# Selection of 16 experts a head with tiles and keys innermost, 17 dense chunks for 19, and sends at two of three token groups

## The chip, the core and the metric

The kernel runs on one core of a Trainium2 chip, as one launch. The core has five engines with a queue each: TensorE (PE; its weight loads are told apart as PEld), VectorE (DVE), ScalarE (ACT), GpSimd (POOL) and SyncE (SP), which here issues most transfers; DMA engines move the data. The metric is the device time of one execution in microseconds (us), the median of several runs; less is better.

## The reference, cut to what matters

Two transformer blocks on 256 tokens of width 1024. The first two thirds of the kernel (attention, convolution, state space, feed-forward, and a second mixer) are not touched. The change lies in the last layer, a feed-forward over 16384 experts, of which every token takes 16 for each of 8 heads:

```python
def retrieve(xb):                       # 128 tokens
    q = (xb @ wq).reshape(PEER_BLOCK, PEER_HEADS, 2, PEER_QDIM // 2)
    s = jnp.einsum('tphq,phkq->tphk', q, keys)          # 2 x 128 keys a head
    top_s, top_i = lax.top_k(s, PEER_TOPK)              # 16 of each 128
    cand = top_s[:, :, 0, :, None] + top_s[:, :, 1, None, :]
    best_s, best_c = lax.top_k(cand.reshape(PEER_BLOCK, PEER_HEADS, 256), PEER_TOPK)
    i1 = jnp.take_along_axis(top_i[:, :, 0], best_c // PEER_TOPK, axis=-1)
    i2 = jnp.take_along_axis(top_i[:, :, 1], best_c % PEER_TOPK, axis=-1)
    idx = i1 * PEER_NKEYS + i2
    g = jax.nn.softmax(best_s, axis=-1)
    act = jax.nn.gelu(jnp.einsum('tpkd,td->tpk', u_tab[idx], xb), approximate=False)
    return jnp.einsum('tpk,tpkd->td', g * act, v_tab[idx])
```

The two take_along_axis lines are what the changed part of `topk` computes: which key number stands at each of the 16 best places.

## The kernel before, in words

An expert's number is 128 times a first key plus a second key. The kernel splits the second keys into D dense ones and 128 - D sparse ones. For the dense keys, u·x is computed for all 128 x D experts and all tokens, two keys to a "chunk"; for the sparse keys only experts that some token chose are gathered. `peer` (L1627) has five stages:

- **Selection** (L1807 to L1816). `head(h)` multiplies the queries of head h on PE (`dense`, L1685: 16 matmuls on 1 MB that SP loads in two halves), multiplies them with the keys (L1708), and ACT copies the scores to the tile sc, of which there are two. `topk` (L1477) then works on DVE alone: per tile of 128 tokens it takes the 16 best of each 128 keys (L1490 to L1494), adds the 16 x 16 pairs (L1497), takes the 16 best (L1503 to L1507), and splits each place into two numbers from 0 to 15 (L1509, L1510). For both tiles and both keys together, L1516 to L1518 turn the places into key numbers: compare each place with 0 to 15 (the table io16, made once on POOL), multiply by the key numbers, add up over the 16. `chunk()` (L1780) is one dense chunk, placed between heads: 16 more matmuls, and a Gelu on ACT.
- **Weights** (L1714): softmax on DVE and ACT, and transposes of idx and of the weights on PE (L1731).
- **Token groups** (L1819): 64 groups of 4 tokens. DVE makes one-hot rows (L1752, L1753), ACT copies one set (L1754), PE multiplies them to the weights of all 16384 experts for each token (L1767, L1769); DVE multiplies those of the keys whose chunk is done into A (L1773) and ACT copies the rest there (L1774). Every tenth group has a chunk. `keep` (L1792) sends eight keys of one tile of A to the DRAM tables Gd (sparse) and Ad (dense), L1802, in SP's queue, each behind the last load.
- **Listing** (`listing`, L1521): the experts with a weight above 0 are numbered, those of the first tile alone, of both, and of the second alone in turn, and turned into lists of 128 to a column, in blocks of four pairs of keys (L1586 to L1597, DVE, ACT and PE in turn). `lims` (L1635) holds for the sparse and the dense keys the column from which the second tile takes part, the column up to which the first does, and the number of columns. The chunks that are left and the other sends come here too.
- **Last stage** (L1854 to L2002): 33 steps of two columns, in an order `seq` (L1847). POOL gathers rows of u and v, or of v alone for dense keys (L1879), and of the tables (L1883). A sparse step transposes u on PE (L1895), splits it into a high and a low part (L1866 ACT, L1867 DVE), multiplies it with the tokens (`first`, 24 matmuls of 256 columns a tile), applies the Gelu (L1908) and weighs it; every step multiplies with v (`second`, L1921, 12 matmuls of 512 columns a tile). A branch ahead of the last steps (L1993) runs `rest` for experts that the lists don't hold.

Within an engine the order of instructions is set by the tile framework's scheduler when the kernel is built, from the order of the code and a timeline that it estimates; SP's queue is in that order too.

Of the kernel before, what the change touches and what calls it, by code (L numbers as in the profile page):

```python
# [12 lines left out]
F16 = mybir.dt.float16  # L13
# [4 lines left out]
OP = mybir.AluOpType  # L18
AX = mybir.AxisListType
# [24 lines left out]
def layout(inp):  # L44
# [16 lines left out]
    g = lambda n: f[n][0]  # L61
    a = {}
# [76 lines left out]
    a["pwq"] = wt(g("peer_wq_2"))  # L139
    a["pkeys"] = g("peer_keys_2").reshape(16, 128, 128).transpose(2, 0, 1).reshape(128, 2048)  # L140
    u = g("peer_u_2").reshape(128, 64, 2, 8, 128)
    a["pu"] = u[:, :19].transpose(1, 4, 2, 3, 0).reshape(19, 128, 2048)
    a["uv"] = np.concatenate([g("peer_u_2"), g("peer_v_2")], axis=1)
    return {k: np.ascontiguousarray(v) for k, v in a.items()}

# [6 lines left out]
class Builder:  # L152
# [1324 lines left out]
    def topk(self, sc, h, tp, I, B):  # L1477

        V = self.V
        tf = tp.tile([128, 2, 2, 16], F16, name="tkf")  # L1480
        c2 = tp.tile([128, 2, 2, 16], F16, name="tkc2")
        z = tp.tile([128, 512], F32, name="tkz")
        for tt in range(2):
            s = sc[:, tt]
            t = tp.tile([128, 2, 16], F32, name="tks")
            ti = tp.tile([128, 2, 16], U32, name="tki")
            for p in range(2):
                x = s[:, p]
                y = tp.tile([128, 128], F32, name="tky")
                V.max(t[:, p, 0:8], x)  # L1490
                V.match_replace(y, t[:, p, 0:8], x, -3e38)
                V.max(t[:, p, 8:16], y)
                V.max_index(ti[:, p, 0:8], t[:, p, 0:8], x)
                V.max_index(ti[:, p, 8:16], t[:, p, 8:16], y)  # L1494
            V.tensor_copy(tf[:, tt], ti)
            cand = tp.tile([128, 16, 16], F32, name="tkc")
            V.tensor_tensor(cand, t[:, 0, :, None].to_broadcast([128, 16, 16]),  # L1497
                            t[:, 1, None, :].to_broadcast([128, 16, 16]), op=OP.add)
            cf = cand.rearrange("p a b -> p (a b)")
            y = z[:, 0:256]  # L1500
            b = B[:, tt, h * 16:(h + 1) * 16]
            bi = tp.tile([128, 16], U32, name="tkbi")
            V.max(b[:, 0:8], cf)  # L1503
            V.match_replace(y, b[:, 0:8], cf, -3e38)
            V.max(b[:, 8:16], y)
            V.max_index(bi[:, 0:8], b[:, 0:8], cf)
            V.max_index(bi[:, 8:16], b[:, 8:16], y)  # L1507
            ci = tp.tile([128, 2, 16], U32, name="tkci")
            V.tensor_scalar(ci[:, 0], bi, 4, None, op0=OP.logical_shift_right)  # L1509
            V.tensor_scalar(ci[:, 1], bi, 15, None, op0=OP.bitwise_and)  # L1510
            V.tensor_copy(c2[:, tt], ci)

        n = [128, 4, 16, 16]
        e = z.bitcast(F16).rearrange("p (a j k) -> p a j k", a=4, j=16)
        c4, t4 = (x.rearrange("p t i k -> p (t i) k") for x in (c2, tf))
        V.tensor_tensor(e, self.io16[:, None].to_broadcast(n), c4[:, :, None, :].to_broadcast(n), op=OP.is_equal)  # L1516
        V.tensor_mul(e, e, t4[:, :, :, None].to_broadcast(n))
        V.tensor_reduce(I[:, :, :, h * 16:(h + 1) * 16].rearrange("p t i k -> p (t i) k"),  # L1518
                        e.rearrange("p a j k -> p a k j"), axis=AX.X, op=OP.add)

    def listing(self, gates, has, place, pc, D, lims):  # L1521

# [104 lines left out]
    def peer(self):  # L1627
        V, S, T, P = self.V, self.S, self.T, self.P
# [2 lines left out]

        D = 38
        lims = ((16, 28, 46), (6, 12, 20))  # L1635
        NS = 128 - D
        self.pts.close()
        self.pst = self.pts.enter_context(self.pool("pst3", 3, PSUM))
# [1 line left out]
        with ExitStack() as es:  # L1640
# [14 lines left out]
            with self.pool("h2x") as tp:  # L1655
                xn = tp.tile([128, 2, 1024], F32, name="xn")
                self.scale_rows(xn, self.x, self.row_r(self.xss))
                for k in range(8):
                    p = self.pst.tile([128, 256], F32, name="t")
# [9 lines left out]
            pc = es.enter_context(self.pool("pc", side="right"))  # L1669
            self.iof = pc.tile([128, 128, 2], F16, name="iof")  # L1670
            P.iota(self.iof, pattern=[[1, 128], [0, 2]], base=0, channel_multiplier=0,
                   allow_small_or_imprecise_dtypes=True)
            self.io16 = pc.tile([128, 16, 16], F16, name="io16")
            P.iota(self.io16, pattern=[[1, 16], [0, 16]], base=0, channel_multiplier=0,
                   allow_small_or_imprecise_dtypes=True)

            it, wt = (pc.tile([128, 128, 2, 2], F16, name=n) for n in ("idxT", "wgtT"))
# [102 lines left out]
            def chunk():  # L1780

                c, n = now["chunk"], now["tokens"]
                now["chunk"] = c + 1
                p = dense(self.I["pu"][c])
                a = A[:, 2 * c:2 * c + 2]
                if n:
                    S.activation(p[:, :, 0:n], p[:, :, 0:n], AF.Gelu)
                    V.tensor_mul(a[:, :, 0:n], a[:, :, 0:n], p[:, :, 0:n])  # L1788
                if n < 256:
                    S.activation(a[:, :, n:], p[:, :, n:], AF.Gelu)  # L1790
# [20 lines left out]
            for h in range(8):  # L1811
                self.topk(sc, h, qp, idx, best)
                if h < 7:
                    sc = head(h + 1)
                chunk()
            weights()  # L1816
            qs.close()
            with self.pool("oh", AHEAD + 1) as op[0]:
                for g in range(256 // NT):  # L1819
                    if g % 10 == 4:  # L1820
                        chunk()
                    group(g * NT, 2 * now["chunk"])
                    now["tokens"] += NT
                    if g % 3 == 2:
                        keep()
            f32 = lambda z: z.rearrange("p a i t -> p (a i t)").bitcast(F32)
            has = f32(wt).rearrange("p (a j) -> p a j", a=2)
# [216 lines left out]
```

## Time and profile before

| what | value |
|---|---|
| median of 3 runs | 1280.24 us (1277.61 to 1283.97) |
| the profiled execution's own time | 1270.43 us |
| its span | 1268.4 us |
| mean granted TensorE clock | 0.968 |
| PE busy | 1177.4 us (93%) |
| DVE busy | 998.0 us (79%) |
| ACT busy | 664.2 us (52%) |
| POOL busy | 171.0 us (13%) |
| moved by DMA | 245.42 MB, mean 193 GB/s |

Busy shares are averages over stages that differ, so they are read stage by stage: a window gives, for a stretch of the span, each engine's busy time, the clock granted to TensorE (1.00 is full speed) and the share of the DMA engines in use. In a timeline each row is one instruction or a run of the same ones: start and length in us, engine, line, operation, what it writes and reads, and, in brackets, how long the engine stood idle before it and what released it. The profiled execution is 9.8 us under the median of the runs.

### The profile page before, as it was taken

Reading aid. Unit: us, or ns where it says so; the run is one execution under the profiler, and the core shown is the slowest. Engines: PE = TensorE matmul, PEld = TensorE weight load, DVE = VectorE, ACT = ScalarE, POOL = GpSimd, SP = SyncE. Lnnn points to the kernel's source line nnn. Section 1 sums busy time; section 2 is a strip of 40 time slices with the busy share of each in tenths; the row PEclk is TensorE's granted clock in tenths of the full one; section 3 lists DMA queues with packets and bytes.
Section 4 is the critical chain, followed back from the end, with each engine's and each line's share of the span. In section 5 each row is a group of like instructions: output and inputs, shape, how many; then the busy total and the mean of one; then the engine's idle time right before and its main releaser. Section 6 shows DMA issues by size and latency. Waiting matters only on the chain. (4 is left out here: it accounts for less than half of the span.)

```text
span 1268.4 us, 20024 instructions
## 1 busy us (share of the span) xinstructions
PE 1177.4 (93%) x7329; PEld 1024.2 (81%) x7329; DVE 998.0 (79%) x2245; ACT 664.2 (52%) x1118; POOL 171.0 (13%) x169
## 2 busy tenths in 40 slices
PE   8999889999999989999999999989883799999986
PEld 7877667789999878897988888879883688888875
DVE  8999988669988877777887599978887677545766
ACT  6665566644644455657644211146656666444653
POOL 3000000000000000000100000000000756444750
PEclk9999899999999999998999999989996799999998
DMA  6651147647899955554335445422849988556761
GB/s 239 209 170 46 35 157 257 225 133 249 264 307 320 311 194 178 170 161 122 117 92 174 136 150 157 142 91 84 226 141 281 394 326 316 202 175 227 272 224 66
DMA packets 92519, 245.42 MB, mean 193 GB/s; under 512 B 7712, under 2 KB 43200, under 8 KB 85888
## 3 DMA queue, kind: packets, MB, share of 16 engines
q1 hardware_dynamic: 79744, 176.72, 43.8%
q0 software_dynamic: 12672, 67.38, 14.6%
q8 instruction: 59, 0.97, 0.3%
q14 instruction: 44, 0.36, 0.1%
HBM read 224.91 MB, written 19.15 MB: 192 GB/s over the span
## 5 line engine op out<-in xcount | busy, mean ns | idle before, releaser
L209 ACT ACTIVATE whi<-raw 128x1024 fp32r<-128x1024 f32 x176 | 185.4, 1058 | 173.0 <-PE g L216 48.4
L210 DVE TENSOR_TENSOR wlo<-raw,whi 128x1024 fp32r<-128x1024 f32 x176 | 214.7, 1223 | 52.6 <-ACT whi L209 51.6
L1695 PE MATMUL g<-hf,raw 128*128 128x256 f32 x864 | 195.3, 384 | 3.1 <-DVE A L1788 1.6
L1695 PEld LDWEIGHTS g<-hf,raw 128*128 128x128 f32 x864 | 163.2, 192 | 24.7 <-ACT A L1790 2.0
L214 PE MATMUL g<-hfh,whi 128*128 128x256 f32 x352 | 100.7, 287 | 2.6 <-DVE ft L879 2.5
L216 PE MATMUL g<-hfh,wlo 128*128 128x256 f32 x352 | 99.0, 286 | 1.6 <-DVE wlo L210 1.6
L215 PE MATMUL g<-hfl,whi 128*128 128x256 f32 x352 | 100.0, 285 | 0.0
L1879 POOL DMA_INDIRECT uv<-in_uv,rowV x46 | 55.0, 1195 | 323.0 <-DVE rowA L1613 281.3
L1867 DVE TENSOR_TENSOR ul<-ut,uh 128x512 fp32r<-128x512 f32 x92 | 61.9, 687 | 36.8 <-ACT uh L1866 36.4
L1867 DVE TENSOR_TENSOR vl<-uv,vh 128x1024 fp32r<-128x1024 f32 x46 | 56.3, 1226 | 27.2 <-ACT vh L1866 25.2
L1866 ACT ACTIVATE uh<-ut 128x512 fp32r<-128x512 f32 x92 | 52.9, 593 | 45.9 <-PE ut L1895 45.0
L214 PE MATMUL g<-vh,ah 128*128 128x512 f32 x168 | 67.9, 408 | 7.1 <-PEq L1993 3.6
L214 PEld LDWEIGHTS g<-hfh,whi 128*128 128x128 f32 x352 | 67.1, 191 | 3.9 <-DVE ft L879 2.7
L215 PE MATMUL us<-ul,h2h 128*128 128x256 f32 x232 | 68.5, 295 | 0.9 <-DVE ul L1867 0.9
L214 PE MATMUL us<-uh,h2h 128*128 128x256 f32 x232 | 68.7, 296 | 0.2 <-ACT uh L1866 0.2
L216 PEld LDWEIGHTS g<-hfh,wlo 128*128 128x128 f32 x352 | 66.4, 190 | 2.3 <-DVE wlo L210 2.2
L215 PEld LDWEIGHTS g<-hfl,whi 128*128 128x128 f32 x352 | 67.0, 190 | 0.0
L215 PE MATMUL g<-vl,ah 128*128 128x512 f32 x168 | 66.5, 398 | 0.0
L216 PE MATMUL us<-uh,h2l 128*128 128x256 f32 x232 | 65.9, 284 | 0.0
L924 DVE SCALAR_TENSOR_TENSOR wmod<-wmod,cc 128x1024 f32<-128x1024 f32 x48 | 58.7, 1223 | 7.9 <-DMA wmod<-in_w_mod 6.7
L1866 ACT ACTIVATE vh<-uv 128x1024 fp32r<-128x1024 f32 x46 | 48.6, 1058 | 30.0 <-PE g L216 27.6
L216 PE MATMUL g<-vh,al 128*128 128x512 f32 x168 | 63.7, 404 | 0.0
(661 smaller groups left out, 3140.2 us busy)
## 6 DMA issues: line engine op xcount, KB each, us to landing
wmod<-in_w_mod SPq DMA_DIRECT2D x48, 512.0 KB, 5.8
raw<-in_ffn_in SPq DMA_DIRECT2D x44, 512.0 KB, 5.4
raw<-in_pu SPq DMA_DIRECT2D x38, 512.0 KB, 3.7
raw<-in_ffn_out SPq DMA_DIRECT2D x22, 512.0 KB, 4.6
Gd<-A SPq DMA_DIRECT2D x22, 512.0 KB, 6.7
raw<-in_w_out SPq DMA_DIRECT2D x16, 512.0 KB, 3.8
raw<-in_pwq SPq DMA_DIRECT2D x16, 512.0 KB, 3.8
raw<-in_w_qkv SPq DMA_DIRECT2D x12, 512.0 KB, 4.4
```

The lines of the kernel that those rows point to most:

```text
L209: self.S.activation(hi, raw, AF.Copy)
L210: self.last_lo = self.V.tensor_sub(lo, raw, hi.bitcast(F32))
L214: a = self.T.matmul(out, ahi, bhi, start=start, stop=False, skip_group_check=True)
L215: self.T.matmul(out, ahi, blo, start=False, stop=False, skip_group_check=True)
L216: b = self.T.matmul(out, alo, bhi, start=False, stop=stop, skip_group_check=True)
L924: i = V.scalar_tensor_tensor(o, w, 1.0, cc[:, j], op0=OP.mult, op1=OP.mult, accum_out=acc)
L1695: T.matmul(p[:, g], w[g][:, k * 128:(k + 1) * 128], hf[:, k], start=k + g == 0, stop=k == 7, skip_group_check=True)
L1866: S.activation(hi, z, AF.Copy)
L1867: V.tensor_sub(lo, z, hi.bitcast(F32))
L1879: P.indirect_dma_start(raw[j], None, vs if k else uv, bass.IndirectOffsetOnAxis(rowV[:, n:n + 1], 0))
```

## The change

It has three parts. In `topk` the tiles of key numbers and of places are laid out with the 16 first and the four pairs of token tile and key side innermost, io16 is stored in full (16 x 16 x 4 numbers), and the sum over the 16 is four adds of halves (512, 256, 128 and 64 numbers) where it was one reduction. D falls from 38 to 34: 17 dense chunks, none after heads 0 and 4, and other list limits. `keep` is called at two of three groups.

```diff
@@ -1477,8 +1477,7 @@
     def topk(self, sc, h, tp, I, B):
 
         V = self.V
-        tf = tp.tile([128, 2, 2, 16], F16, name="tkf")
-        c2 = tp.tile([128, 2, 2, 16], F16, name="tkc2")
+        tf, c2 = (tp.tile([128, 16, 2, 2], F16, name=n) for n in ("tkf", "tkc2"))
         z = tp.tile([128, 512], F32, name="tkz")
         for tt in range(2):
             s = sc[:, tt]
@@ -1492,7 +1491,7 @@
                 V.max(t[:, p, 8:16], y)
                 V.max_index(ti[:, p, 0:8], t[:, p, 0:8], x)
                 V.max_index(ti[:, p, 8:16], t[:, p, 8:16], y)
-            V.tensor_copy(tf[:, tt], ti)
+            V.tensor_copy(tf[:, :, tt].rearrange("p j a -> p a j"), ti)
             cand = tp.tile([128, 16, 16], F32, name="tkc")
             V.tensor_tensor(cand, t[:, 0, :, None].to_broadcast([128, 16, 16]),
                             t[:, 1, None, :].to_broadcast([128, 16, 16]), op=OP.add)
@@ -1508,15 +1507,16 @@
             ci = tp.tile([128, 2, 16], U32, name="tkci")
             V.tensor_scalar(ci[:, 0], bi, 4, None, op0=OP.logical_shift_right)
             V.tensor_scalar(ci[:, 1], bi, 15, None, op0=OP.bitwise_and)
-            V.tensor_copy(c2[:, tt], ci)
-
-        n = [128, 4, 16, 16]
-        e = z.bitcast(F16).rearrange("p (a j k) -> p a j k", a=4, j=16)
-        c4, t4 = (x.rearrange("p t i k -> p (t i) k") for x in (c2, tf))
-        V.tensor_tensor(e, self.io16[:, None].to_broadcast(n), c4[:, :, None, :].to_broadcast(n), op=OP.is_equal)
-        V.tensor_mul(e, e, t4[:, :, :, None].to_broadcast(n))
-        V.tensor_reduce(I[:, :, :, h * 16:(h + 1) * 16].rearrange("p t i k -> p (t i) k"),
-                        e.rearrange("p a j k -> p a k j"), axis=AX.X, op=OP.add)
+            V.tensor_copy(c2[:, :, tt].rearrange("p k a -> p a k"), ci)
+
+        n = [128, 16, 16, 4]
+        e = z.bitcast(F16).rearrange("p (j k a) -> p j k a", j=16, a=4)
+        c4, t4 = (x.rearrange("p k t i -> p k (t i)") for x in (c2, tf))
+        V.tensor_tensor(e, self.io16, c4[:, None].to_broadcast(n), op=OP.is_equal)
+        V.tensor_mul(e, e, t4[:, :, None].to_broadcast(n))
+        for m in (8, 4, 2):
+            V.tensor_add(e[:, 0:m], e[:, 0:m], e[:, m:2 * m])
+        V.tensor_add(I[:, :, :, h * 16:(h + 1) * 16].rearrange("p t i k -> p k (t i)"), e[:, 0], e[:, 1])
 
     def listing(self, gates, has, place, pc, D, lims):
 
...
 
 
 
-        D = 38
-        lims = ((16, 28, 46), (6, 12, 20))
+        D = 34
+        lims = ((16, 28, 48), (6, 10, 18))
         NS = 128 - D
         self.pts.close()
         self.pst = self.pts.enter_context(self.pool("pst3", 3, PSUM))
@@ -1670,8 +1670,8 @@
             self.iof = pc.tile([128, 128, 2], F16, name="iof")
             P.iota(self.iof, pattern=[[1, 128], [0, 2]], base=0, channel_multiplier=0,
                    allow_small_or_imprecise_dtypes=True)
-            self.io16 = pc.tile([128, 16, 16], F16, name="io16")
-            P.iota(self.io16, pattern=[[1, 16], [0, 16]], base=0, channel_multiplier=0,
+            self.io16 = pc.tile([128, 16, 16, 4], F16, name="io16")
+            P.iota(self.io16, pattern=[[1, 16], [0, 64]], base=0, channel_multiplier=0,
                    allow_small_or_imprecise_dtypes=True)
 
             it, wt = (pc.tile([128, 128, 2, 2], F16, name=n) for n in ("idxT", "wgtT"))
@@ -1812,7 +1812,8 @@
                 self.topk(sc, h, qp, idx, best)
                 if h < 7:
                     sc = head(h + 1)
-                chunk()
+                if h % 4:
+                    chunk()
             weights()
             qs.close()
             with self.pool("oh", AHEAD + 1) as op[0]:
@@ -1821,7 +1822,7 @@
                         chunk()
                     group(g * NT, 2 * now["chunk"])
                     now["tokens"] += NT
-                    if g % 3 == 2:
+                    if g % 3:
                         keep()
             f32 = lambda z: z.rearrange("p a i t -> p (a i t)").bitcast(F32)
             has = f32(wt).rearrange("p (a j) -> p a j", a=2)
```

The input `pu` holds 17 chunks where it held 19. Of the 33 steps of the last stage two differ: step 18 (dense keys) works on the second tile alone where it worked on both, and step 29 (second tile) is a sparse step where it was a dense one.

DVE, the end of the sixth head in the selection (tk names are tiles of `topk`, sc the scores, idx the key numbers). Before:

```order
L1503 MAX best<-tkc 128x8
L1504 MATCH_REPLACE tkz<-best,tkc 128x256
L1506 MAX_INDEX tkbi<-best,tkc 128x8
L1505 MAX best<-tkz 128x8
L1507 MAX_INDEX tkbi<-best,tkz 128x8
L1509 TENSOR_SCALAR tkci<-tkbi 128x16
L1510 TENSOR_SCALAR tkci<-tkbi 128x16
L1511 CAST tkc_7621<-tkci 128x32
L1516 TENSOR_TENSOR tkz<-io_6989,tkc_7621 128x1024
L1517 TENSOR_TENSOR tkz<-tkz,tkf 128x1024
L1518 TENSOR_REDUCE idx<-tkz 128x4x16
L1490 MAX tks<-sc 128x8 x2
```

The next head (L1490) begins behind the reduction. The same head now:

```order
L1515 TENSOR_TENSOR tkz<-io_6989,tkc_7592 128x1024
L1493 MAX_INDEX tki<-tks,tky 128x8
L1496 TENSOR_TENSOR tkc<-tks 128x256
L1516 TENSOR_TENSOR tkz<-tkz,tkf 128x1024
L1502 MAX best<-tkc 128x8
L1489 MAX tks<-sc 128x8 x2
L1518 TENSOR_TENSOR tkz<-tkz 128x512
L1494 CAST tkf<-tki 128x2x16
L1505 MAX_INDEX tkbi<-best,tkc 128x8
L1490 MATCH_REPLACE tky<-tks,sc 128x128
L1518 TENSOR_TENSOR tkz<-tkz 128x256
L1492 MAX_INDEX tki<-tks,sc 128x8 x2
```

Before, the product (L1517) and the reduction (L1518) stand right behind each other and behind what they need; now work of the next head (L1489, L1490, L1492 among it) stands between the product (L1516) and each of the adds (L1518).

PE, the end of the selection, from the difference of the two orders (L1695 are dense matmuls, L1708 the key matmuls of a head, L1731 the transposes of idx and of the weights):

```order
 L1708 MATMUL t<-keys,pq 128x128 x4
-L1695 MATMUL g<-hf,raw 128x256 x32
+L1695 MATMUL g<-hf,raw 128x256 x16
 L1708 MATMUL t<-keys,pq 128x128 x4
 L1695 MATMUL g<-hf,raw 128x256 x32
 L1708 MATMUL t<-keys,pq 128x128 x4
-L1695 MATMUL g<-hf,raw 128x256 x32
-L1708 MATMUL t<-keys,pq 128x128 x4
-L1695 MATMUL g<-hf,raw 128x256 x45
+L1695 MATMUL g<-hf,raw 128x256 x47
 L1731 MATMUL t<-ident,idx 128x128 x4
 L1731 MATMUL t<-ident,best 128x128 x2
```

The chunk behind head 4 is gone; that behind head 0 is gone further up, where 27 dense matmuls became 12. From the first key matmuls to L1731 there were 244 dense matmuls and are 214, and behind L1731 there were 152 and are 150.

## Rows read from the trace of the kernel before

**Rows 1.** Windows by stage: engines' busy us, clock, DMA share, GB/s.
```profile
715.00:730.00 15.00, 15.00 (x75) 13.33 (x74) 14.83 (x78) 3.09 (x5) 0.00 (x0) 1.00 0.53 170
820.00:832.00 12.00, 6.45 (x30) 5.43 (x30) 11.48 (x48) 1.88 (x3) 0.00 (x0) 0.90 0.41 128
832.00:845.00 13.00, 13.00 (x79) 11.36 (x78) 8.67 (x18) 3.81 (x8) 0.00 (x0) 0.83 0.27 82
845.00:945.00 100.00, 94.79 (x966) 85.98 (x965) 85.54 (x188) 66.75 (x135) 0.00 (x0) 1.00 0.48 139
957.00:990.00 33.00, 10.68 (x129) 9.38 (x129) 22.57 (x70) 26.20 (x36) 6.99 (x7) 0.54 1.01 293
1100.00:1150.00 50.00, 50.00 (x330) 45.41 (x329) 26.82 (x38) 23.16 (x38) 22.31 (x20) 1.00 0.59 203
```

**Rows 2.** Timeline of DVE, the selection's first instruction: start, us, idle before, releaser.
```profile
714.67 0.49 DVE L1490 MAX8 tks<-sc 128x8 f32<-128x128 f32 x2 [10.41 <-ACT sc L1711]
```

**Rows 3.** Timeline of PE around the end of the selection.
```profile
806.00 19.59 PE L1695 MATMUL g<-hf,raw 128*128 128x256 f32 x90
831.14 1.11 PE L1731 MATMUL t<-ident,idx 128*128 128x128 f32 x4 [5.55 <-DVE idx L1518]
...
832.48 9.94 PE L1695 MATMUL g<-hf,raw 128*128 128x256 f32 x36
```

**Rows 4.** Groups of lines, 712 to 835 us: shapes, count, busy us, mean ns.
```profile
L1518 DVE TENSOR_REDUCE idx<-tkz 128x64 f32<-128x1024 f16 x8 | 15.9, 1987 | 0.1
L1517 DVE TENSOR_TENSOR tkz<-tkz,tkf 128x1024 f16<-128x1024 f16 x8 | 9.8, 1220 | 0.1
```

**Rows 5.** Lines L1753 and L1594 alone: count, ns min/median/max, first and last start.
```profile
L1753 DVE TENSOR_TENSOR ow<-o,wgtT x64: 684/686/696, 835.0 to 942.8; 128x1024 f16<-128x1024 f16 x64
...
L1594 DVE TENSOR_TENSOR lw<-oc,pj x17: 207/350/352, 957.7 to 986.5; 128x368 f16<-128x368 f16 x11, 128x160 f16<-128x160 f16 x4, 128x92 f16<-128x92 f16 x1, 128x120 f16<-128x120 f16 x1
```

**Rows 6.** Timeline of DVE, ends of the first three heads.
```profile
730.32 1.98 DVE L1518 TENSOR_REDUCE idx<-tkz 128x64 f32<-128x1024 f16 x1
...
741.89 1.22 DVE L1517 TENSOR_TENSOR tkz<-tkz,tkf 128x1024 f16<-128x1024 f16 x1
743.03 0.42 DVE L1503 MAX8 best<-tkc 128x8 f32<-128x256 f32 x1
...
743.75 1.98 DVE L1518 TENSOR_REDUCE idx<-tkz 128x64 f32<-128x1024 f16 x1
745.65 0.17 DVE L1495 CAST tkf<-tki 128x32 f16<-128x32 uint32 x1
...
755.90 2.00 DVE L1518 TENSOR_REDUCE idx<-tkz 128x64 f32<-128x1024 f16 x1
```

**Rows 7.** Timeline of DVE, ends of the sixth and the seventh head.
```profile
798.57 2.01 DVE L1518 TENSOR_REDUCE idx<-tkz 128x64 f32<-128x1024 f16 x1
...
811.62 0.69 DVE L1516 TENSOR_TENSOR tkz<-io,tkc 128x1024 f16<-128x1024 f16 x1
812.35 1.23 DVE L1517 TENSOR_TENSOR tkz<-tkz,tkf 128x1024 f16<-128x1024 f16 x1
813.61 2.00 DVE L1518 TENSOR_REDUCE idx<-tkz 128x64 f32<-128x1024 f16 x1
```

**Rows 8.** Timeline of PE inside the last stage.
```profile
1137.65 0.40 PE L216 MATMUL g<-vh,al 128*128 128x512 f32 x1
1137.88 1.04 PE L1895 MATMUL ut<-ident,uv 128*128 128x128 f32 x8
1138.68 0.36 PE L214 MATMUL us<-uh,h2h 128*128 128x256 f32 x1
...
1139.11 0.28 PE L214 MATMUL us<-uh,h2h 128*128 128x256 f32 x1
1139.23 0.28 PE L215 MATMUL us<-ul,h2h 128*128 128x256 f32 x1
```

**Rows 9.** The page, DMA issues: KB each, median us to landing.
```profile
raw<-in_pu SPq DMA_DIRECT2D x38, 512.0 KB, 3.7
```

More of the change, by code (lines that the diff above doesn't have):

```diff
@@ L141, in layout @@
     u = g("peer_u_2").reshape(128, 64, 2, 8, 128)
-    a["pu"] = u[:, :19].transpose(1, 4, 2, 3, 0).reshape(19, 128, 2048)
+    a["pu"] = u[:, :17].transpose(1, 4, 2, 3, 0).reshape(17, 128, 2048)
     a["uv"] = np.concatenate([g("peer_u_2"), g("peer_v_2")], axis=1)
```

## Prediction

> **What bounds the kernel now.** I read the windows by stage first: they show which engine is full where the change acts. In the selection of the experts (715 to 820 us) the reader is to see PE and DVE full at the same time: 15.00 and 14.83 of 15 us [rows 1]. The timeline of DVE and that of PE then say which of the two ends the stage. DVE starts on the first head's scores at 714.67 after a wait for ACT [rows 2]. PE issues its last dense matmuls at about 825.4 (90 records from 806.00, 0.216 us apart; one matmul is two records, so 0.43 us), stands still for 5.55 us, and goes on at 831.14, released by DVE's write of idx [rows 3]. So DVE ends the selection after 831.1 - 714.7 = 116.5 us, and PE alone would have ended it 5.6 us earlier: cutting one engine's work without the other's buys at most that. Behind it the token groups (845 to 945) have PE at 94.8 of 100 us, the listing (957 to 990) has ACT at 26.2 of 33 with PE mostly waiting, and the last stage has PE at 50.0 of 50 [rows 1]. Those three engines price whatever the change moves there.
>
> **Key numbers on DVE.** Each of 8 heads loses a product with a repeated innermost operand, 1220 ns (L1517), and a reduction that reads with a stride, 1987 ns (L1518) [rows 4]. In their place come a product whose innermost four numbers are distinct, and adds of 512, 256, 128 and 64 numbers. The nearest row for the product is L1753: 1024 f16 numbers, its third operand repeated in a middle dimension and only two numbers long innermost, 686 ns. The adds lie on the line between it and L1594 (368 f16 numbers, 350 ns) [rows 5]: 0.52 ns a number and a fixed 0.16 us, so 0.42, 0.29 and 0.22 us; the last writes f32 and is priced at the slow rate, 0.22. Durations: 3.21 us go and 1.84 come, 1.37 a head, 11.0 us in all. But an instruction that does not need the one ahead of it starts before that one has ended: L1503 stands 1.14 us after the start of L1517, and L1495 1.90 after L1518 [rows 6], about 0.08 less than their durations. By starts 3.04 us go and 1.44 come: 1.60 a head, 12.8 in all.
>
> The Trainium skill ("VectorE: DVE Perf Modes", The DRAIN you can't avoid) says that after an operation the next does not start until the pipe is empty; by that the sum here would be the 11.0 of the durations. The trace disagrees (743.03 against 741.89 + 1.22). The same page's tier table gives a reduction one number per cycle, which with its fixed term would make an estimated 1.22 us for 1024 numbers and leave under 7 us of gain; the trace has 1.99 for this strided one, and the measurement decides.
>
> **The order on DVE.** Whether an instruction needs the one ahead is settled by the order, and that changes too. In the second half of the heads the end of a head runs alone, each instruction waiting for its forerunner's end: L1517 starts 0.73 after L1516, L1518 1.26 after L1517. From the sixth head's reduction to the seventh's it takes 15.04 us [rows 7]; from the second's to the third's, where the next head's work stands between, 12.15 [rows 6]. In the new order the next head's work stands between for nearly all heads. I walked both orders with these rows: an instruction starts at its forerunner's start plus the distance above, or 0.02 us after the end of what it needs. The old order gives 116.2 us (the trace 116.5), the new one 99.5. I take the difference, **16.7 us**. Bounds: 11.0 (no change in the filling) and 24: the first head's reduction begins 15.65 us after the first MAX8, the next two follow at 12.8 on the mean [rows 6], and 14.0 + 7 x 11.2 + 0.2 = 92.6 if every head did so.
>
> **Two chunks fewer on PE.** Between the first key matmuls and the transposes of idx 214 dense matmuls now stand instead of 244: 30 x 0.43 = 12.9 us, so PE would be done at 825.4 - 12.9 = 812.5 and DVE at 831.1 - 16.7 = 814.4. DVE stays last, by 2 us. Without this part DVE's gain would stop at 5.6. By the same distances every head's scores are there before DVE asks for them, by 2.9 us at the least (second head). PE's standstill shrinks from 5.6 to 2 us; the granted clock at its end is 0.90 and 0.83 and the 36 records from 832.48 take 9.94 instead of 7.8 us [rows 1, 3]. That 2.2 us may come back; I count nothing and keep it as a bound.
>
> **Token groups.** 150 dense matmuls are left for after the selection instead of 152: -0.9 us on PE, which bounds there. Every group's product on DVE gets 16 numbers shorter and ACT's copy 16 longer; DVE has 14 of 100 us free and ACT 33 [rows 1], so 0. If PE's order did not cover it, it would be some 0.02 us x 64 = 1 us either way.
>
> **Sends at two of three groups.** SP's order has the first tile's 12 sends of Gd in one piece before and now. Two sends of Ad move ahead of them; 17 to 19 sends still stand behind the last group, 19 before. One load of the last chunk now queues behind a send of Ad that waits for a product on DVE; that chunk's matmuls stand behind the last group in PE's order, so it is not late. The listing hides the sends as it did (ACT 26.2 of 33 us, DMA share 1.01) [rows 1]: 0. Without that cover a send of 512 KB would cost some 1.8 us at the 293 GB/s there.
>
> **Lists and the last stage.** The listing keeps 17 blocks; the short ones (one pair, three pairs) swap places, and widths go 46 to 48 and 20 to 18: 0, within 0.5 us, hidden by nothing since ACT bounds. In the last stage a step on both tiles loses one, 12 matmuls of 512 columns at 0.23 = -2.8 us, and a step that only gathers v becomes one that also gathers, transposes and multiplies u: 16 transposes at 0.80 for 8, 24 matmuls of 256 columns at 0.12, and about 0.5 for the switches between kinds and two transposes more [rows 8]: +5.0. Together **+2.3 us** on a full PE. Ends: 1.7 without the switches; 5.0 if the 2.8 were hidden anyway. The larger gather needs 1 MB more, with DMA at a share of 0.59 [rows 1]: 0. POOL's table of numbers grows from 256 to 1024, well before its first use: 0.
>
> **Sum.** -16.7 - 0.9 + 2.3 = **-15.3 us**. The profiled execution took 1270.43 us (span 1268.4 and 2.0 around it) and would take 1255.1; the median of the runs shown is 1280.24 (1277.61 to 1283.97), 9.8 above the profiled one, so I set the difference against that: **1264.9 us**. A measurement of this kernel can tell about 0.5%, 6.4 us, from no change.
>
> **Rivals.** (A) The above. (B) The filling does not come about, because scores arrive late or the chip pairs instructions less well than the rows do: DVE gains 11 to 12.8, total -10.5: 1269.7. For it: the margin of PE is only 2 us. Against: the measured 12.15 of the interleaved heads. (C) The product and adds run at L1517's rate, 1.04 ns a number: product 1.22, adds 0.69, 0.42, 0.29, 0.22 us; the walk gives 107.5, a gain of 8.7, total -7.3: 1273. Decides: whether four distinct innermost numbers suffice for the rate of L1753, which has two [rows 5]. The Trainium skill (the same page, What auto-detection actually checks) asks for every tensor 16-bit with step one for the doubled rate; whether a repeated middle dimension breaks this, no sentence there says, and L1753 speaks for the fast case. (D) Slower: the lists overflow. Counting the reference's selection on its inputs, with weights rounded as the kernel rounds them, the first tile fills 27.5 of 28 columns and both tiles 47.2 of 48 in the sparse part, 9.7 of 10 and 17.0 of 18 in the dense one. From the first expert over a limit the branch before the last steps runs its 128 passes, with 94 x 2 + 34 loads of 512 KB one after the other: at 3.7 us each [rows 9] 820 us more, above 2000. Before, the margins were of the same size and the branch was not taken. (E) That the third part doesn't do what it says: the sends keep their place in SP's order, which is why they stand at 0 above; it is part of A.
>
> **Numbers.** A 0.62, B 0.22, C 0.13, D 0.03. A is faster; B mostly (0.18 of 0.22, the rest within 0.5%); C falls about half on each side. Faster 0.86, same 0.11, slower 0.03. The range takes in C with 3 us of scatter above, 1276, and below A with the upper bound of the filling and 1.7 for the last stage, 1257.
>
> **What would show it.** In the changed kernel's lines, right: the product, L1516, near 0.69, the first add near 0.42; idx finished about 99 us after the first MAX8; PE's standstill before the transposes near 2 us; 23 transposing steps turned 24 and the end some 2 us later relative to the start of the last stage. Wrong: L1516 at 1.2 (C); DVE waiting for scores (B); instructions of L1944 in the trace (D); or a token-group stage that grows by as much as the selection shrinks.

## The result and the profile after

The changed kernel took **1268.0 us** (median of 4 runs, 1267.8 to 1270.0), the kernel before beside it 1282.1 (4 runs, 1277.6 to 1287.6): ratio 0.990, 95% interval 0.987 to 0.993. That is 14.1 us less, 1.1%, where 15.3 had been forecast; the 1264.9 forecast was set against the first three runs of before, at 1280.2, and 1268.0 lies inside the range given.

The profiled execution of the changed kernel lasted 1269.97 us, only 0.5 less than that of [rows 1]. Times differ from chip to chip: in the runs below the kernel before has medians of 1271.1, 1272.3 and 1282.1 us on three chips. So stages are compared here between two executions from one chip, one of each kernel (1269.9 and 1255.3 us of span; runs before_again and after_again below). Windows by stage of the second profile of the changed kernel (window and length, then busy us of PE, PEld, DVE, ACT, POOL, the granted clock, DMA share, GB/s):

```profile
718.00:733.00 15.00, 15.00 (x79) 13.43 (x78) 14.83 (x80) 3.56 (x5) 0.00 (x0) 1.00 0.53 161
816.00:826.00 10.00, 9.86 (x66) 8.84 (x67) 7.47 (x17) 2.48 (x5) 0.00 (x0) 1.00 0.42 134
828.00:928.00 100.00, 93.90 (x960) 84.64 (x958) 83.90 (x187) 67.01 (x135) 0.00 (x0) 1.00 0.49 142
940.00:972.00 32.00, 11.23 (x128) 9.74 (x128) 22.43 (x69) 26.42 (x36) 5.50 (x6) 0.52 0.96 273
1100.00:1150.00 50.00, 50.00 (x319) 44.84 (x318) 25.31 (x36) 21.68 (x35) 22.67 (x21) 1.00 0.55 194
```

The same engines bound the same stages as in [rows 1]; only the window behind the selection looks different, with the clock at 1.00. The timeline of PE there, to be laid beside [rows 3]:

```profile
799.68 15.05 PE L1695 MATMUL g<-hf,raw 128*128 128x256 f32 x69
816.14 0.66 PE L1731 MATMUL t<-ident,idx 128*128 128x128 f32 x4 [1.41 <-DVE idx L1519]
816.85 7.94 PE L1695 MATMUL g<-hf,raw 128*128 128x256 f32 x36
```

PE stands still for 1.4 us in place of 5.5, and the 36 records (18 matmuls) behind take 7.9 in place of 9.9. The groups of lines on DVE (shapes, count, busy us, mean ns) give the prices that [rows 4, 5] had to stand in for:

```profile
L1516 DVE TENSOR_TENSOR tkz<-tkz,tkf 128x1024 f16<-128x1024 f16 x8 | 5.5, 684 | 0.1
L1518 DVE TENSOR_TENSOR tkz<-tkz 128x512 f16<-128x512 f16 x8 | 3.3, 406 | 0.0
L1518 DVE TENSOR_TENSOR tkz<-tkz 128x256 f16<-128x256 f16 x8 | 2.2, 278 | 0.0
L1519 DVE TENSOR_TENSOR idx<-tkz 128x64 f32<-128x64 f16 x8 | 2.0, 252 | 0.0
L1518 DVE TENSOR_TENSOR tkz<-tkz 128x128 f16<-128x128 f16 x8 | 1.7, 207 | 0.0
```

Where the time went, between marks read from the timelines of the two executions on one chip (us):

| from, to | before | changed | difference | forecast |
|---|---|---|---|---|
| start, first MAX8 (L1490, now L1489) | 716.04 | 716.76 | +0.72 | untouched |
| first MAX8, PE's transposes of idx (L1731) | 116.46 | 99.38 | **-17.08** | -16.7 |
| L1731, first matmul of the token groups (L1767) | 11.27 | 8.48 | **-2.79** | 0, bound -2.2 |
| L1767, last product into A (L1773) | 102.73 | 102.93 | +0.20 | -0.9 |
| L1773, end of the lists (last rowA) | 44.81 | 44.79 | -0.02 | 0 |
| last rowA, first Gelu of gathered scores | 9.92 | 11.39 | **+1.47** | 0 |
| first Gelu, first gy | 236.74 | 239.21 | +2.47 | +2.3 with the next line |
| first gy, end of the span | 31.97 | 32.36 | +0.39 | |
| sum | 1269.94 | 1255.30 | -14.64 | -15.3 |

The first line is scatter: that part is the same code, and the first MAX8 came between 714.6 and 719.5 us in the profiles of this study.

### The profile page after: what moved, and what is told of

Read it like the earlier page. It is cut to its first block, busy times and chain, and to the rows that moved or that the text cites. A ratio compares the mean times of both kernels' runs of the same rounds, so it can differ in the third digit from the quotient of the medians.

```text
span 1268.2 us, 19978 instructions
## 1 busy us (share of the span) xinstructions
PE 1169.2 (92%) x7295; PEld 1013.8 (80%) x7295; DVE 983.1 (78%) x2274; ACT 665.8 (53%) x1121; POOL 170.9 (13%) x169
## 5 line engine op out<-in xcount | busy, mean ns | idle before, releaser
L1695 PE MATMUL g<-hf,raw 128*128 128x256 f32 x800 | 180.2, 381 | 3.8 <-ACT A L1790 2.1
L1695 PEld LDWEIGHTS g<-hf,raw 128*128 128x128 f32 x800 | 149.1, 190 | 23.2 <-ACT A L1790 2.7
L1868 DVE TENSOR_TENSOR ul<-ut,uh 128x512 fp32r<-128x512 f32 x96 | 64.7, 686 | 45.1 <-ACT uh L1867 29.2
L215 PE MATMUL g<-hfl,whi 128*128 128x256 f32 x352 | 99.5, 283 | 0.0
L1880 POOL DMA_INDIRECT uv<-in_uv,rowV x48 | 58.0, 1208 | 195.7 <-DMA g<-gd 149.0
L214 PE MATMUL us<-uh,h2h 128*128 128x256 f32 x240 | 72.1, 300 | 3.4 <-ACT uh L1867 3.2
L215 PE MATMUL us<-ul,h2h 128*128 128x256 f32 x240 | 71.2, 297 | 0.4 <-issue 0.3
L216 PE MATMUL us<-uh,h2l 128*128 128x256 f32 x240 | 68.7, 286 | 0.0
L924 DVE SCALAR_TENSOR_TENSOR wmod<-wmod,cc 128x1024 f32<-128x1024 f32 x48 | 58.5, 1220 | 10.4 <-DMA wmod<-in_w_mod 7.3
L216 PE MATMUL g<-vh,al 128*128 128x512 f32 x164 | 61.9, 403 | 0.0
```

Source lines behind the costliest of these rows:

```text
L214: a = self.T.matmul(out, ahi, bhi, start=start, stop=False, skip_group_check=True)
L215: self.T.matmul(out, ahi, blo, start=False, stop=False, skip_group_check=True)
L216: b = self.T.matmul(out, alo, bhi, start=False, stop=stop, skip_group_check=True)
L924: i = V.scalar_tensor_tensor(o, w, 1.0, cc[:, j], op0=OP.mult, op1=OP.mult, accum_out=acc)
L1695: T.matmul(p[:, g], w[g][:, k * 128:(k + 1) * 128], hf[:, k], start=k + g == 0, stop=k == 7, skip_group_check=True)
L1868: V.tensor_sub(lo, z, hi.bitcast(F32))
```

## The experiments

Twelve runs. Four shared one chip (before_again, after_again, numbers_only, lists_only; before at 1271.1 us, 25 runs), four a second (keep_undone, chunks_moved, reduce_kept, from_18; before at 1272.3, 18 runs), four a third (1282.1, 11 runs). Ratios are to before on the same chip.

**The two kernels again.** No edit: before_again and after_again are the two kernels as they were.

> The kernel before, unchanged. Its timed runs lie at 1277.6 to 1287.6 us, its profiled execution at 1270.4. Theory S (one execution differs from another at one place, the start of the last stage, where the first gathers of u run with the DMA engines full): the selection takes 116 us again (first MAX8 to the last write of idx, within 1 us), the token groups 102.7, and what differs from the first profile by several us is the stretch from the last write of A to the first Gelu of gathered scores (54.7 us in the first profile; 55 to 65 here). Rival U (the executions differ everywhere by a little, by the granted clock): every stage is longer by the same share, about 1% for 1282. Rival V (the first profile of before is simply what the kernel takes): all stages within 1 us of the first profile.

> The changed kernel, unchanged: 1268 us, 14 below before on the same chip. In its first profile the last stage starts 7.5 us late against before (62.2 us from the last write of A to the first Gelu of gathered scores, 54.7 in before). Theory S: the selection takes 99.3 us again, and that stretch comes out at 54 to 60, as in before: the lateness was one execution's. Rival L (something of the change delays the first gathers: two sends of Ad less behind the groups, the gathers set off 1.5 us later): it is 62 us again, and 54 to 56 in the second profile of before.

Measured: 1272.2 us, ratio 1.0006 [0.9992, 1.002], and 1256.9 us, ratio **0.989** [0.987, 0.991]: 14.2 us less, the first result over again. The stages of before repeat to within 0.2 us, the stretch from the last product into A to the first Gelu included (54.7 both times), so S and U fall for this kernel: its first profile is what it takes on such a chip (V). For the changed kernel that stretch is 56.2 now and was 62.2: the 6 us do not belong to the change, as S has it, and of L only 1.5 us are left, which the section on the prediction takes up.

**The numbers alone.** Before, with this part of the change only:

```diff
-        n = [128, 4, 16, 16]
...
+        n = [128, 16, 16, 4]
...
+        for m in (8, 4, 2):
+            V.tensor_add(e[:, 0:m], e[:, 0:m], e[:, m:2 * m])
```

> Before with the change of the key numbers on DVE alone (product and adds with tiles and keys innermost); 19 dense chunks, the old lists and sends. By the sum of the prediction: DVE would need 99.5 us, but PE with 244 dense matmuls ends 5.6 us before the old DVE, so the selection goes from 116.4 to about 111 us, PE has no standstill before the transposes of idx, and the 2 us of lower clock behind it come back: -5.6 to -8 us, 1274 to 1276 where before is at 1282. Product L1516 0.69 us, first add 0.42. Rival (PE is not the limit, it fits its dense matmuls to what DVE leaves): the selection takes 100 us and the run is 15 to 19 us faster, with the rest of the dense matmuls later at no cost.

Measured: 1264.0 us, ratio 0.995 [0.993, 0.997]: **-7.1 us**. Ends of the selection, DVE's last add and PE's timeline:

```profile
822.67 0.27 DVE L1519 TENSOR_TENSOR idx<-tkz 128x64 f32<-128x64 f16 x1
```

```profile
807.43 19.16 PE L1695 MATMUL g<-hf,raw 128*128 128x256 f32 x88
826.43 0.60 PE L1731 MATMUL t<-ident,idx 128*128 128x128 f32 x4
```

DVE is done at 822.9, PE goes on to 826.4 without a wait: now PE ends the stage, 110.3 us after the first MAX8 (716.11), as worked out (111). The rival is out. But DVE itself needed 106.8 us, not 99.5: the numbers alone take only 9.6 us off DVE. Of the 7.3 us too much only 0.6 is a wait, for the last head's scores; the rest lies in the order of the instructions, which the next two runs take up.

**The lists alone.** Before, with this part only:

```diff
-        D = 38
-        lims = ((16, 28, 46), (6, 12, 20))
+        D = 34
+        lims = ((16, 28, 48), (6, 10, 18))
...
-                chunk()
+                if h % 4:
+                    chunk()
```

> Before with two dense chunks fewer and the lists that suit them alone (D = 34, a chunk behind six of the heads); old key numbers and old sends. By the sum of the prediction: DVE bounds the selection, 116 us as before, PE's standstill before the transposes grows from 5.6 to about 18 us; token groups -0.9, last stage +2.3, and the longer standstill may cost some 1 to 2 us more of low clock: +1 to +4 us, 1283 to 1286 where before is at 1282. Rival (fewer dense chunks are the gain, the sends and the last stage gain by them): -3 us or better.

Measured: 1268.6 us, ratio 0.997 [0.996, 0.999]: **-2.5 us** where +1 to +4 was expected. The last stage is longer (3.2 us from the first Gelu to the end, 2.3 forecast), but the selection is shorter by 6.5 us (idx finished 109.9 us after the first MAX8) without one instruction less on DVE, and PE's standstill is 8.1 us where 18 were expected. PE's timeline:

```profile
799.77 18.08 PE L1695 MATMUL g<-hf,raw 128*128 128x256 f32 x83
825.98 1.12 PE L1731 MATMUL t<-ident,idx 128*128 128x128 f32 x4 [8.14 <-DVE idx L1518]
```

**Two chunks moved, nothing else.** Is it the smaller tables, or that fewer chunks stand between the heads?

```diff
             self.topk(sc, h, qp, idx, best)
             if h < 7:
                 sc = head(h + 1)
-            chunk()
+            if h % 4:
+                chunk()
```

> Before with one edit: a dense chunk behind six of the heads, not eight; 19 chunks in all, so two of them move behind the selection; old key numbers, old lists, old sends. In the run with the lists alone the selection fell from 116.4 to 109.9 us although no instruction on DVE changed. Theory O (with fewer dense matmuls planned between the heads, the next head's instructions are laid between those of the one before on DVE): here the selection takes 110 us too (a walk of this kernel's order on DVE gives 110.3), and the two chunks cost 16 matmuls x 0.43 x 2 = 13.8 us behind it: +6 to +9 us against before; -6 if the listing hides them. Rival T (it came from the smaller tables and lists): the selection takes 116 us and the run is 8 to 14 us slower.

Measured: 1277.0 us, ratio 1.0035 [1.0016, 1.0054], +4.7 us, a little under the +6 to +9 expected; the selection takes 109.9 us, and the stretch from the transposes to the first token group is 1.4 us shorter than in before_again, which the expectation had not counted. **O is shown, T falls.** The timeline of DVE says how. In before, at the end of the seventh head, each instruction waits for its forerunner's end (before_again):

```profile
812.97 0.69 DVE L1516 TENSOR_TENSOR tkz<-io,tkc 128x1024 f16<-128x1024 f16 x1
813.70 1.23 DVE L1517 TENSOR_TENSOR tkz<-tkz,tkf 128x1024 f16<-128x1024 f16 x1
814.96 2.01 DVE L1518 TENSOR_REDUCE idx<-tkz 128x64 f32<-128x1024 f16 x1
```

In chunks_moved, with the same instructions in all, the next head's stand between:

```profile
808.32 0.67 DVE L1516 TENSOR_TENSOR tkz<-io,tkc 128x1024 f16<-128x1024 f16 x1
808.91 0.08 DVE L1494 MATCH_VALUE_LOAD tki<-tks,tky 128x8 f32 x1
808.99 0.29 DVE L1494 FIND_INDEX8 tki<-tks,tky 128x8 uint32<-128x128 f32 x1
809.19 0.41 DVE L1497 TENSOR_TENSOR tkc<-tks 128x256 f32<-128x256 f32 x1
809.51 1.22 DVE L1517 TENSOR_TENSOR tkz<-tkz,tkf 128x1024 f16<-128x1024 f16 x1
810.64 0.42 DVE L1503 MAX8 best<-tkc 128x8 f32<-128x256 f32 x1
810.98 0.47 DVE L1490 MAX8 tks<-sc 128x8 f32<-128x128 f32 x2
811.37 1.98 DVE L1518 TENSOR_REDUCE idx<-tkz 128x64 f32<-128x1024 f16 x1
```

From one head's reduction to the next it takes 14.6 to 15.6 us in the last four heads of before, 11.4 to 14.3 here. The moved chunks cost 13.4 us behind the token groups (last product into A to the end of the lists: 58.2 us against 44.8), near the 13.8 of their matmuls, but part of it is not matmuls: PE's longest single wait there is for the last chunk's load, in the waits of PE from 925 to 1000 us (us in total, times, longest):

```profile
PE g L1695 <- DMA raw<-in_pu: 7.6, 1, 7.6
```

**One reduction in place of the adds.**

```diff
-        for m in (8, 4, 2):
-            V.tensor_add(e[:, 0:m], e[:, 0:m], e[:, m:2 * m])
-        V.tensor_add(I[:, :, :, h * 16:(h + 1) * 16].rearrange("p t i k -> p k (t i)"), e[:, 0], e[:, 1])
+        V.tensor_reduce(I[:, :, :, h * 16:(h + 1) * 16].rearrange("p t i k -> p k (t i)"),
+                        e.rearrange("p j k a -> p k a j"), axis=AX.X, op=OP.add)
```

> The changed kernel with one reduction over the 16 key positions in place of the four adds; the product stays in the new form. If the reduction takes the 1.99 us of before, it costs 1.91 in place of 0.85 from start to start, 1.06 a head; the walk of this order on DVE gives 107.2 us for the selection in place of 99.6: +7 to +8 us against the changed kernel, some 7 below before. If the reduction runs at one number a cycle (some 1.2 us), it is +2. If it reads slower with its longer stride, up to +15.

Measured: 1264.4 us, ratio 0.993 [0.991, 0.995], 8 below before; the selection takes 106.4 us, 7.1 more than with the adds. So of the 17.1 us about 7 are the adds' part. The group of the line:

```profile
L1517 DVE TENSOR_REDUCE idx<-tkz 128x64 f32<-128x1024 f16 x8 | 15.2, 1904 | 0.0
```

1.90 us in place of the 1.99 of [rows 4], with a stride four times as long. From its start to the next one's it takes 1.82 us; the four adds in after_again, in the heads whose ends are filled, 0.76 together (0.32, 0.20, 0.12 and 0.12). Four adds beat one reduction. The Trainium skill ("VectorE: DVE Perf Modes", Rules for kernel authors) tells one to keep the count of chained operations low, and also to expect a reduction at one number per cycle and to restructure it: here the two pull apart. The run bears out the advice to restructure, but not the one number per cycle, by which the prediction had estimated 1.22 us.

**The sends.** The changed kernel with the third part undone, on two chips, and on the third chip beside the changed kernel itself (after_third, no edit):

```diff
-                    if g % 3:
+                    if g % 3 == 2:
                         keep()
```

> The changed kernel with the first tile's sends called for at one of three groups again (the numbers and the lists stay). By the prediction the sends are worth 0: this run stands within 3 us of the changed kernel (about 14 us below before), and from the last write of A to the first Gelu of gathered scores it takes 56 us as there. What the two halves give alone (numbers -7, lists -2.5, measured) adds up to -9.6 only; so a rival is that the sends give the missing 4 to 5 us: then this run stands 9 to 10 us below before. The other reading is that numbers and lists are worth more together, since alone each is stopped by the other engine: then 14 us, with the selection at 99.3.

> The changed kernel with the sends called for at one of three groups, as before, again. If the sends are worth nothing (the prediction): within 2 us of the changed kernel beside it. Its first run stood 17.5 us below before, the changed kernel 14.2 on another occasion; if the earlier sends cost that difference, this one is 3 us or more below the changed kernel, and its last stage starts earlier by that much.

> The changed kernel, unchanged, beside the next one on the same chip: 14 to 16 us below before. First Gelu of gathered scores 56 us after the last write of A, or up to 62 as in its first profile.

Measured: keep_undone 1254.8 us, ratio 0.986 [0.983, 0.989]; keep_undone_2 1266.7, ratio 0.989 [0.986, 0.991], beside after_third at 1266.4, ratio 0.988 [0.986, 0.991]. On one chip the two differ by 0.3 us, with intervals of some 3 us either way: **the sends are worth nothing that these runs can tell**. The rival that they give 4 to 5 us is out: keep_undone stands 17.5 us below before, and the selection takes 99.3 us without them too. That the earlier sends cost 3 us, as this 17.5 beside the 14.2 of another chip suggested, did not repeat in the medians. What numbers and lists give beyond the sum of their runs is mostly the 3.5 us that PE alone held up in numbers_only. From the last product into A to the first Gelu keep_undone took 54.9 us, not the 56 expected; keep_undone_2 took 57.0 where after_third took 61.9, though their medians agree, so one execution's stretch decides nothing here. That the sends were moved shows in their line (SP's sends of Ad: count, ns min/median/max, first and last start), here for after_third

```profile
L1802 SPq DMA_DIRECT2D Ad<-A x11: 377/574/3290, 875.7 to 956.6; - x11
```

and for keep_undone_2

```profile
L1802 SPq DMA_DIRECT2D Ad<-A x10: 359/926/2047, 904.5 to 958.2; - x10
```

Counted from the first MAX8 of each (714.63 and 717.76), the first goes 25.7 us earlier, but the last 1.5 us later: earlier calls did not finish the sends of Ad sooner. The end of the lists is the same 44.8 us behind the groups.

**A shorter list for both tiles.** The count that had served for rival D has 18.98 columns of the first tile alone where the lists use 16:

```diff
-        lims = ((16, 28, 48), (6, 10, 18))
+        lims = ((18, 28, 48), (6, 10, 18))
```

> The changed kernel with the sparse list's tile-0-only part one step longer (18 columns in place of 16; with 17 dense chunks the first tile's own experts fill 18.98 columns by a count of the selection). One step of the last stage is then for one tile in place of two: 24 matmuls of 256 columns at 0.12, 12 of 512 at 0.23 and two transposes less, 2.9 + 2.8 + 0.2 = 5.9 us on a PE that is full there: 6 us below the changed kernel, 20 below before. Rival (the gathers of u bound that step, so that the work taken away was hidden): 0 to -3.

> The changed kernel with 18 columns for tile 0 alone in the sparse list. The first run's profile has the last stage (first Gelu to the first gy) at 234.3 us against 239.2, 4.9 less where 5.9 was worked out: so 5 us below the changed kernel beside it.

> The same with the sends of before: the second pair on the question of the sends. Worth nothing: within 2 us of the one with the new sends; cost as in the first runs: 3 us below it, and the fastest of all, 23 to 25 us below before.

Measured: from_18 1250.3 us, ratio **0.982** [0.980, 0.984]; from_18_2 1262.1, ratio 0.985 [0.982, 0.987]; from_18_old_sends (the same with `g % 3 == 2`) 1263.3, ratio 0.986 [0.983, 0.988]. In from_18 first Gelu and first gy are

```profile
983.81 0.38 ACT L1909 ACTIVATE us<-us 128x256 f32<-128x256 f32 x1
```

```profile
1218.08 0.69 DVE L2009 TENSOR_TENSOR gy<-g,g 128x512 f32<-128x512 f32 x1 [3.26 <-DVEq L1994]
```

234.3 us apart, 4.9 less than in after_again and 5.2 less than in keep_undone on its own chip (5.9 worked out). On the third chip the same stretch is 3.1 us shorter in from_18_2 than in after_third, and 5.6 in from_18_old_sends than in keep_undone_2. Beside after_third the median of from_18_2 is 4.3 us lower (5 expected); the intervals overlap a little, so it is the stage that shows it, and the rival of 0 to -3 is out on the chip of the first run. This version is below both kernels. The second pair says the same of the sends: 1.3 us more with those of before, not 3 less.

## Why the prediction was right, point by point

- **What bounds.** Right: DVE ended the selection in before, PE was done 5.5 us ahead of it, and with DVE alone made faster PE ends it (numbers_only).
- **Prices on DVE.** The product takes 0.684 us (0.69 taken), the adds 0.41, 0.28, 0.21 and 0.25 (0.42, 0.29, 0.22, 0.22). Rival C is out: four distinct numbers innermost run like L1753. The section of the Trainium skill that the prediction sets against its rows ("VectorE: DVE Perf Modes", The DRAIN you can't avoid) goes on to say that a next instruction that is not held starts earlier. So the early start of L1503 in [rows 6] does not contradict it.
- **The walk.** 99.5 us for the new order; 99.3 measured. **But the 16.7 stood under the wrong heading.** The text took the better filling as a companion of the new key numbers, and let the two chunks act on PE alone. The selection, as DVE sees it, takes 116.4 us in before, 106.8 with the numbers, 109.9 with the chunks thinned out, 99.3 with both: -9.6 and -6.5 by themselves, and chunks_moved shows the second with no other edit. The walk came out because it was made on the finished order, which held both.
- **Two chunks fewer.** Right that without them DVE's gain would stop at 5.6 (6.1 measured, numbers_only) and that 2 us of standstill would be left (1.4).
- **The clock, kept as a bound.** Mis-sized at 0: the 36 records behind the transposes fell from 10.1 us in before_again to 7.9, and with the rest of that stretch -2.79 came back. The granted clock is 0.74 there on the mean

```profile
832.00:844.00 12.00, 11.50 (x46) 9.80 (x47) 7.73 (x16) 1.95 (x4) 0.00 (x0) 0.74 0.15 45
```

  and 1.00 now (816 to 826 us, shown above). The 0.74 is a mean of two levels, as the last section shows.
- **Token groups.** -0.9 forecast, +0.2 measured: what two matmuls fewer save does not show.
- **Lists, "0, within 0.5 us".** This step failed. The listing as a whole lasts as long, but the first gather needs the sparse list alone, and that one got longer (48 columns for 46, and three pairs in its last block for one; this cause is read from the code, no run has it alone). In before_again, DVE's numbers of the sparse list and POOL's first gather:

```profile
981.23 0.19 DVE L1609 CAST rowV<-ta 128x46 int32<-128x46 f32 x1
```

```profile
982.32 1.12 POOL L1879 DMA_INDIRECT uv<-in_uv,rowV  x1 [281.30 <-DMA gf<-in_rows]
```

  that is 34.7 and 35.8 us after the last product into A (946.50); in after_again

```profile
963.90 0.18 DVE L1609 CAST rowV<-ta 128x48 int32<-128x48 f32 x1
```

```profile
964.98 1.12 POOL L1880 DMA_INDIRECT uv<-in_uv,rowV  x1 [148.98 <-DMA gf<-in_rows]
```

  36.4 and 37.4 us after it (927.55). The first gather is 1.6 us later, and the first Gelu 1.5. lists_only has the same 37.4, numbers_only the old 36.0 (973.75 after 937.80), so the gather's delay goes with the lists. That it costs the Gelu as much is not shown: keep_undone has the gather after 37.4 us too, but the Gelu after 54.9, beside 54.7 in before_again, 55.6 in numbers_only, 56.2 in after_again and 56.5 in lists_only.
- **Last stage.** +2.3 forecast (its own terms, 5.0 less 2.8, give 2.2), +2.9 measured (2.47 and 0.39).
- **Sends.** 0, confirmed on one chip within some 3 us. **Overflow** (D): no instruction of L1944 in the trace. **DVE waiting for scores** (B): its only listed wait in the selection is the first, 10.4 us, ahead of the first MAX8; with all chunks in place, in numbers_only, one of 0.6 us came.

The sum of the terms came within 0.7 us of the two profiles from one chip, partly by luck: the clock's +2.8 paid for the late gathers, the token groups and the last stage.

## What to carry to other kernels

When work is taken from one engine inside a scheduled program, ask what it does to the order on the others: here two chunks less on PE gave DVE 6.5 us by letting independent instructions stand between dependent ones. A strided f16 reduction may be cheaper as a tree of dense adds, though that is more instructions (here 0.76 us from start to start for 1.82). A list made in two parts is finished, for its first reader, when the first part is; a balance that keeps the whole can still delay that reader (here its first gather, by 1.6 us).

## What was not expected of the hardware

- **Chips differ at one place.** Each chip was used on one occasion, so the two are not told apart. On the third chip the stretch from the end of the lists to the first Gelu took 17.1 to 17.3 us in three of four profiles (12.2 in keep_undone_2) where it is 9.9 to 12.3 in those of the first two, and the stretch from there to the first gy was longer by 6 to 8 us in all four (245.3 in after_third, 239.2 in after_again). All that lies ahead, from the first MAX8 to the end of the lists, agreed to 0.1 us. ACT in after_third:

```profile
979.39 0.60 ACT L1867 ACTIVATE uh<-ut 128x512 fp32r<-128x512 f32 x1 [1.32 <-issue]
984.47 0.60 ACT L1867 ACTIVATE uh<-ut 128x512 fp32r<-128x512 f32 x1 [4.48 <-remote]
...
987.32 0.39 ACT L1909 ACTIVATE us<-us 128x256 f32<-128x256 f32 x1 [0.82 <-issue]
```

  The idle time ends at nothing that the profile names (issue and remote name no engine and no queue), while the DMA engines are full (share 1.01 from 970 to 982). The first profile of the changed kernel shows the same (17.4 us), which is why it is no shorter than the first of before. What holds the engines there was not settled.
- **The clock after a standstill.** With 8.1 us of standstill before the transposes in lists_only the first token group came 11.1 us after them, with 5.5 in before_again 11.3, with 1.4 in after_again 8.5, with none in numbers_only 8.4; in chunks_moved, with 8.1 again, 9.9. Little or no wait gives the time back; among longer ones the loss, 1.4 to 2.8 us against 8.5, is not in step with the wait's length. The granted clock, read 0.1 us by 0.1 us, says what it is in step with. In after_again and numbers_only it is 1.00 (2.4 GHz) all through. In the others it falls during the standstill to 0.50 (1.2 GHz) and comes back only after PE works again: 5.7 us after the start of the transposes in before_again, 5.3 in lists_only, 2.9 in chunks_moved, 2.8 in reduce_kept (7.2 us of standstill, 9.85 to the first token group). The loss is half of that time in each: 2.8, 2.6, 1.5 and 1.4 us. Why the clock comes back sooner in two of them was not settled.
